# Modulation rows stored through one transposed 32 x 128 tile, and an issue-order edge on the weighted activations

## The chip, the cores and the metric

The kernel runs on one core of a Trainium2 chip. The metric is the device time of one execution in microseconds (us): 3135.5 us is the median of three runs before the change (3133.11 to 3138.17). The core has a matrix engine (TensorE, PE in the profile, with its weight loads as PEld), a vector engine (DVE), an activation engine (ACT), GpSimd (POOL) and a queue engine that mostly starts DMAs (SP). DMAs are also started from ACT and from POOL. Each engine works through its own instructions in the order in which they were queued, and the engines wait for each other through semaphores.

## The reference, cut to what matters

Two transformer blocks over 512 tokens of width 1024. The part that the change touches is the modulation of the first block: a vector `c` is turned into six vectors of 1024 numbers, three for the attention part and three for the expert part. The late four (`gt1`, `sh2`, `sc2`, `gt2`) are used after the attention.

```
mod_x = (silu(c) @ w_mod + b_mod)
sh1, sc1, gt1, sh2, sc2, gt2 = split(mod_x, 6)
px = split(modulate(rms_norm(x, norm1), sh1, sc1) @ w_in, ...)   # projections q, k, v, f, ...
x = x + gt1 * (concat([na_x, hg_x]) @ w_out)                       # attention and recurrence
x = x + gt2 * peer_ffn(modulate(rms_norm(x, norm2), sh2, sc2), ...)
```

`peer_ffn` picks 16 of 16384 experts for each token and head, and sums `gelu(u . h) * g * v` over them. The kernel computes it for 384 tokens as dense products with all experts, 128 chunks of 128 experts, with the weights `g` spread into a table of zeros; 128 tokens go through gathers.

## The kernel before, in words

`mixer` is the first stage. `mix_norm` normalises the input and makes the early modulation. Then `weave(self.project_na(first), self.late_mods())` runs two generators against each other: `project_na` projects q, k and v (each weight tile `w` of 512 KB or 256 KB comes by an SP DMA, ACT rounds it into `wh` at L148, DVE makes the rest `wl` at L149, PE multiplies at L122), and `late_mods` (L464 to L476) makes the four late vectors out of 32 chunks of 128 numbers. One chunk is `mod_chunk` (L326 to L333): an SP DMA of 512 KB into a buffer of the same ring `w` (four buffers, shared with the projection weights), one product with sum on DVE (L332, 1.22 us) and one small addition (L333).

A late vector lies as a column tile of 128 partitions x 8 numbers. It is also needed as a row (to be spread over all partitions later), so after every eight chunks `keep_rows` (L364 to L366) stores the column tile into a DRAM row `Rd[n]`, from POOL:

```
self.nc.gpsimd.dma_start(self.Rd[n].rearrange("(k p) -> p k", p=128), vec)
```

The target is contiguous along p and the source along k, so that no two neighbours of the source are neighbours in the target: one store is 1024 runs of 4 bytes. The rows are read back at L371 (`rows_of`), much later.

After the weave `lower_bounds` (L432 to L446) makes two small tables on DVE and ACT, and `project_f` (L592, matmuls at L611) is woven with `na_tiles` (`na_scores` L866 with the bias load L882, the score matmuls L887 and L890, the bias addition L892, the maximum L894 and the exponential L896; `na_transpose` L903; the value products).

What sets the order: the tile framework traces the instructions in program order and a scheduler places them on each engine; `with self.after(ins)` adds an edge that keeps what is traced inside behind `ins` on that engine's queue, without a wait. The expert loop at the end of `peer` calls `operands(e)` (L1376) for each chunk of 128 experts: the stored activations `act` are multiplied by the weights `Wr` on DVE (L1390), split into `sh` (ACT, L133) and `sl` (DVE, L135), and the weights `v` are split into `vh` and `vl` by the same helper `split` (L129 to L136).

Of the kernel before, what the change touches and what calls it, by code (L numbers as in the profile page):

```python
# [7 lines left out]
F32 = mybir.dt.float32  # L8
# [4 lines left out]
OP = mybir.AluOpType  # L13
# [3 lines left out]
D = 1024  # L17
S = 512
C = 256
KC = D // 128  # L20
# [6 lines left out]
GROUP = 8  # L27
# [24 lines left out]
def run(gen):  # L52
    while True:
        try:
            next(gen)
        except StopIteration as e:
            return e.value
# [7 lines left out]
def weave(*gens):  # L65

    at = [[0.0, i, g] for i, g in enumerate(gens)]
    while at:
        cur = min(at, key=lambda x: (x[0], x[1]))
        try:  # L70
            cur[0] += next(cur[2])
        except StopIteration:
            at.remove(cur)
# [18 lines left out]
class Net:  # L92
# [37 lines left out]
    def split(self, pool, src, shape, name, low=None, bufs=None):  # L130
        kw = {"bufs": bufs} if bufs else {}
        hi = pool.tile(shape, FR, name=name + "h", **kw)
        self.nc.scalar.activation(hi, src, AF.Copy)  # L133
        lo = pool.tile(shape, FR, name=name + "l", **kw)
        (low or self.nc.vector).tensor_tensor(out=lo, in0=src, in1=hi, op=OP.subtract)  # L135
        return hi, lo  # L136

    def rows2(self, src, k0, c0, n):
# [216 lines left out]
        self.nc.vector.tensor_tensor(out=m[:, n], in0=b[:, :4].rearrange("p (j i) -> p j i", j=2),  # L355
                                     in1=self.bm[:, n:n + KC + 1:KC].unsqueeze(2).to_broadcast([128, 2, 2]), op=OP.add)

    def gain_of(self, vec, scale, j, name):

        o = self.g.tile([128, KC], F32, name=name)  # L360
        self.nc.vector.scalar_tensor_tensor(o, scale[:, :, j], 1.0, self.gains[:, vec], op0=OP.add, op1=OP.mult)
        return o

    def keep_rows(self, n, vec):  # L364

        self.nc.gpsimd.dma_start(self.Rd[n].rearrange("(k p) -> p k", p=128), vec)  # L366

    def rows_of(self, n, name, pool):

# [5 lines left out]
    def mixer(self):  # L375
        y = self.pool("y")
        self.Y = y.tile([128, 4, 512], F32, name="Y")
        self.open_stream()
        pj = self.pool("pj")
        hh = pj.tile([128, KC, C + S], FR, name="hh")  # L380
        hl = pj.tile([128, KC, C + S], FR, name="hl")
        self.project_setup(pj, hh, hl)
        first = self.proj(self.p['win'], 0, 512, [self.xs])
        for n in self.mix_norm(hh, hl):
            if n % 2:
                next(first)
        m = self.pool("mixf", "right")
        self.F = m.tile([128, 2, 6, 512], F32, name="F")
        self.mixn = m = self.pool("mixn", "right")
        self.q2 = m.tile([128, 8, S], FR, name="q2")  # L390
        self.k2 = m.tile([128, 8, S + C], FR, name="k2")
        self.ql = m.tile([128, 4, S], FR, name="ql")
        self.V = m.tile([128, 9, 512], F32, name="V")
        weave(self.project_na(first), self.late_mods())
        with self.after(self.last_v):
            self.lower_bounds()
        self.shut("mp")
        na = self.pool("na", "right")
        weave(self.project_f(), self.na_tiles(na))
        self.shut("na")  # L400
        self.shut("mixn")
        m = self.pool("mixi", "right")
        self.I = m.tile([128, 6, 512], F32, name="I")
        self.G = m.tile([128, 4, 512], F32, name="G")
        self.hq = m.tile([128, 4, S], F32, name="hq")
        self.load_bounds()
        q = self.project_q()
        for _ in range(2):
            next(q)
        with self.after(self.last_exp):  # L410
            self.gates()
        run(q)
        self.shut("lbt")
        run(self.project_g())
        hg = self.pool("hg", "right")
        kv = []
        values = self.project_i()
        next(values)
        with self.after(self.log_table(self.last_sig)):
            weave(values, self.hg_keys_decayed(hg, kv))  # L420
        self.shut("pj")
        self.shut("st")
        self.hg_chunks(hg, kv)
# [38 lines left out]
                nc.vector.tensor_tensor(out=f, in0=f, in1=self.lb[:, d:d + 1].to_broadcast([128, 3, 512]), op=OP.add)  # L462

    def late_mods(self):  # L464
        self.Rd = self.tc.dram_tile([4, D], F32, name="Rd")
        for j, name in ((2, "gt1"), (3, "sh2"), (4, "sc2"), (5, "gt2")):
            t = self.g.tile([128, KC, 1], F32, name=name)
            setattr(self, name, t)
            for k in range(KC):
                self.mod_chunk(j, t[:, k], k)  # L470
                yield 3.0
            if j in (2, 3, 5):
                self.keep_rows((2, 3, 5).index(j) + (j > 2), t[:, :, 0])
            if j == 4:
                self.a2 = self.gain_of(1, t, 0, "a2")
                self.keep_rows(1, self.a2)  # L476

    def mix_norm(self, hh, hl):

# [548 lines left out]
    def peer(self):  # L1028
        nc, p = self.nc, self.p
        hh, hl = self.h2  # L1030
        mv = ([hh[:, k] for k in range(KC)], [hl[:, k] for k in range(KC)])
        first = self.proj_first(self.ws, mv, lambda i: self.normed_half(i, [(hh, hl, self.a2)], 1e-6, self.sh2[:, :, 0]))
        self.finish = None
        for name in ("wo", "st", "hca", "y", "pn"):
            self.shut(name)
# [56 lines left out]
        for t in range(4):  # L1092
            sq = self.sp.tile([128, 2], F32, name="ssp")
            for h in range(2):
                b = banks[t - 1][h] if t else self.accg[:, h * 512:(h + 1) * 512]
# [5 lines left out]
            r = self.rstd(sq, 1e-6)  # L1101
# [276 lines left out]
    def operands(self, pm, e, mv):  # L1378

        nc, p = self.nc, self.p  # L1380
        n, j = divmod(e, GROUP)
        if j == 0:
            self.Wr = self.Wn
        if e < AHEAD:
            a = pm.tile([128, TD], F32, name="act", bufs=3)
            nc.sync.dma_start(a, self.Ad[e])
        else:
            a = self.hidden(pm, self.rows_u(e), mv)
        a3 = a.rearrange("p (b t) -> p b t", t=WT)
        self.anchor = nc.vector.tensor_tensor(out=a3, in0=a3, in1=self.Wr[:, :, e % GROUP], op=OP.mult)  # L1390
        sh, sl = self.split(pm, a, [128, TD], "s", bufs=TAIL + OPS_LAG)
        v = self.st.tile([128, 2, 512], F32, name="w", bufs=WBUFS)
        nc.sync.dma_start(v.rearrange("p a b -> p (a b)"), p['V'][e])
        if j >= WLATE and e < 128 - GROUP:
            self.spread_rows(pm, n + 1, j - WLATE)
        vh, vl = self.split(pm, v, [128, 2, 512], "v", bufs=TAIL + OPS_LAG)
        return sh, sl, vh, vl
# [462 lines left out]
```

## Time and profile before

| | |
|---|---|
| runs before, median (lowest to highest) | 3135.5 us (3133.11 to 3138.17) |
| profiled execution, device time | 3140.31 us |
| its span, first to last instruction | 3138.5 us |
| PE busy | 2946.8 us, 94% of the span |
| DVE busy | 1890.9 us, 60% |
| ACT busy | 1271.9 us, 41% |
| POOL busy | 442.8 us, 14% |
| granted TensorE clock, mean | 0.969 |

The profiled execution is one execution; its own time is 4.8 us over the median, and the span is 1.8 us less than its time. Busy shares are means over stages of different kinds. The slices of the profile's page show PE at 90% or more nearly everywhere, and the slices in which it falls are short stages of their own; the first three (0 to 235 us) read 7, 8 and 7, and in the third the granted clock reads 8.

### The profile page before, as it was taken

The numbers are of one execution on the slowest core, as the hardware profiler recorded it, in microseconds if no ns is written. First come the engines' busy times: TensorE is split into PE (matmuls) and PEld (weight loads), VectorE is DVE, ScalarE is ACT, GpSimd is POOL, SyncE is SP. The second block draws the span as 40 slices with busy tenths as digits, with TensorE's granted clock in tenths as the row PEclk, the third lists the DMA queues.
The fourth block names the chain that finished last, engine by engine and source line by source line (L and its number), as shares of the span: only waits on it lengthen the run. The fifth ranks groups of instructions, "written<-read, shape, count | busy, mean of one in ns | idle before, by whom it ended". The sixth has DMA issues, their size and how long they took to land.

```text
span 3138.5 us, 42272 instructions
## 1 busy us (share of the span) xinstructions
PE 2946.8 (94%) x16009; PEld 2528.4 (81%) x16009; DVE 1890.9 (60%) x3640; ACT 1271.9 (41%) x2275; POOL 442.8 (14%) x402
## 2 busy tenths in 40 slices
PE   7879898999999999988898888899999999999998
PEld 5668797889899999967677777778888887788887
DVE  5644477639999966678788886544433245543323
ACT  4223464344366677633333323433323234433222
POOL 2200000100211210144454441000000000000000
PEclk9989999999999999999999999999999999999999
DMA  6832202334676776899999996222333222133332
GB/s 244 188 83 72 88 8 68 111 118 135 228 235 220 250 248 238 273 360 372 351 379 370 358 373 220 65 75 89 101 95 100 95 88 68 48 88 100 94 101 81
DMA packets 259148, 539.89 MB, mean 172 GB/s; under 512 B 21632, under 2 KB 136576, under 8 KB 254592
## 3 DMA queue, kind: packets, MB, share of 16 engines
q1 hardware_dynamic: 198368, 347.92, 34.9%
q0 software_dynamic: 36992, 134.25, 11.9%
q10 hardware_dynamic: 23584, 55.03, 4.7%
q8 instruction: 125, 2.05, 0.3%
q14 instruction: 79, 0.65, 0.1%
HBM read 487.02 MB, written 50.09 MB: 171 GB/s over the span
## 4 chain that ended last, share of the span: by engine, by line
PE 59%; DVE 18%; DMA 8%; issue 2%; ACT 1%; SPq 1%; POOL 0%; ACTq 0%; DVEq 0%; POOLq 0%
PE bank L122 57%; DMA act<-Ad 4%; DMA w<-in_V_dram 2%; DVE wl L1351 2%; DVE vl L135 2%; DVE gr L1163 2%; DVE accg L1168 2%; DMA gr<-in_Un_dram,iu 1%; DVE sl L135 1%; PE bank L611 1%; DVE act L1390 1%; PE bank L1499 1%; DVE tmp L1241 1%; DVE eq L1280 1%; DVE eq L1282 1%
## 5 line engine op out<-in xcount | busy, mean ns | idle before, releaser
L122 PE MATMUL bank<-hh,wl 128*128 128x512 f32 (+2 forms) x2304 | 840.5, 365 | 36.3 <-DVE wl L1351 18.4
L122 PE MATMUL bank<-hh,wh 128*128 128x512 f32 (+2 forms) x2304 | 845.4, 368 | 22.6 <-ACT wh L1350 8.8
L122 PE MATMUL bank<-hl,wh 128*128 128x512 f32 (+2 forms) x2304 | 834.4, 362 | 1.4 <-DVE hl L272 0.8
L149 DVE TENSOR_TENSOR wl<-w,wh 128x1024 fp32r<-128x1024 f32 (+2 forms) x280 | 297.1, 1062 | 644.6 <-ACT wh L148 637.6
L148 ACT ACTIVATE wh<-w 128x1024 fp32r<-128x1024 f32 (+2 forms) x280 | 257.4, 920 | 769.3 <-PE bank L122 596.8
L122 PEld LDWEIGHTS bank<-hh,wl 128*128 128x128 f32 x2304 | 439.3, 191 | 95.4 <-DVE wl L1351 26.7
L122 PEld LDWEIGHTS bank<-hh,wh 128*128 128x128 f32 x2304 | 438.7, 191 | 74.8 <-ACT wh L148 9.9
L122 PEld LDWEIGHTS bank<-hl,wh 128*128 128x128 f32 x2304 | 439.3, 191 | 50.8 <-DVE hl L272 1.5
L122 PE MATMUL bank<-vh,sh 128*128 128x512 f32 x768 | 251.5, 410 | 61.8 <-ACT sh L133 61.8
L1144 POOL DMA_INDIRECT gr<-in_Un_dram,iu x128 | 198.8, 1553 | 760.0 <-DVE accg L1168 523.5
L122 PE MATMUL bank<-vh,sl 128*128 128x512 f32 x768 | 245.8, 402 | 1.3 <-DVE sl L135 1.2
L122 PE MATMUL bank<-vl,sh 128*128 128x512 f32 x768 | 246.7, 403 | 0.0
L122 PEld LDWEIGHTS bank<-vh,sh 128*128 128x128 f32 x768 | 149.2, 198 | 102.4 <-ACT sh L133 72.9
L133 ACT ACTIVATE vh<-w 128x1024 fp32r<-128x1024 f32 x128 | 134.6, 1056 | 193.6 <-DMA w<-in_V_dram 169.5
L1351 DVE TENSOR_TENSOR wl<-w,wh 128x1024 fp32r<-128x1024 f32 x128 | 155.8, 1217 | 89.1 <-ACT wh L1350 89.0
L1350 ACT ACTIVATE wh<-w 128x1024 fp32r<-128x1024 f32 x128 | 135.3, 1058 | 153.9 <-PE bank L122 147.1
L122 PEld LDWEIGHTS bank<-vh,sl 128*128 128x128 f32 x768 | 148.6, 195 | 36.8 <-DVE sl L135 5.4
L122 PEld LDWEIGHTS bank<-vl,sh 128*128 128x128 f32 x768 | 149.3, 196 | 35.3 <-DVE vl L135 2.9
L1144 POOL DMA_INDIRECT gr<-in_V_dram,iv x128 | 161.0, 1258 | 83.9 <-DVE accg L1168 37.4
L216 POOL TENSOR_TENSOR r<-r,mhalf 128x1 f32<-128x1 f32 x37 | 21.9, 595 | 1014.1 <-DVE r L215 1007.3
L1168 DVE SCALAR_TENSOR_TENSOR accg<-gr,wt,accg 128x1024 f32<-128x1024 f32 x127 | 162.1, 1276 | 0.1
L135 DVE TENSOR_TENSOR vl<-w,vh 128x1024 fp32r<-128x1024 f32 x128 | 155.6, 1216 | 8.7 <-ACT vh L133 8.7
(367 smaller groups left out, 4719.2 us busy)
## 6 DMA issues: line engine op xcount, KB each, us to landing
w<-in_U_dram SPq DMA_DIRECT2D x128, 512.0 KB
w<-in_V_dram SPq DMA_DIRECT2D x128, 512.0 KB
w<-in_wgu_dram SPq DMA_DIRECT2D x84, 512.0 KB
Wd<-W ACTq DMA_DIRECT2D x24, 1024.0 KB
Wr<-Wd SPq DMA_DIRECT2D x96, 256.0 KB
w<-in_wdown_dram SPq DMA_DIRECT2D x44, 512.0 KB
Ad<-act ACTq DMA_DIRECT2D x116, 192.0 KB
act<-Ad SPq DMA_DIRECT2D x116, 192.0 KB
```

Source lines behind the costliest of these rows:

```text
L122: return self.nc.tensor.matmul(out, a, b, start=start, stop=stop)
L133: self.nc.scalar.activation(hi, src, AF.Copy)
L135: (low or self.nc.vector).tensor_tensor(out=lo, in0=src, in1=hi, op=OP.subtract)
L148: self.nc.scalar.activation(hi[:, :, :n], w[:, :, :n], AF.Copy)
L149: (self.low or self.nc.vector).tensor_tensor(out=lo[:, :, :n], in0=w[:, :, :n], in1=hi[:, :, :n], op=OP.subtract)
L611: nc.tensor.matmul(o, x[k], y[:, kk, :256], start=k == 0 and i == 0 and t % 2 == 0, stop=k == KC - 1 and i == 2, skip_group_check=True)
L1144: nc.gpsimd.indirect_dma_start(out=t, out_offset=None, in_=table, in_offset=bass.IndirectOffsetOnAxis(ap=idx, axis=0))
L1163: nc.vector.scalar_tensor_tensor(t, t, 1.0, self.h0, op0=OP.mult, op1=OP.mult, accum_out=dots[:, h, k:k + 1])
L1168: nc.vector.scalar_tensor_tensor(acc, t, wt[:, h, k:k + 1], acc, op0=OP.mult, op1=OP.add)
L1241: nc.vector.match_replace(tmp, val[:, 0:8], src, -3e38)
L1350: nc.scalar.activation(uh, w, AF.Copy)
L1351: nc.vector.tensor_tensor(out=ul, in0=w, in1=uh, op=OP.subtract)
```

## The change: one store of 32 rows, and an edge in the expert loop

The four late vectors become four slices of one tile `late` (128 partitions x 4 x 8). The four stores of 128 x 8 are gone. After the weave, `keep_rows` turns the whole tile with one transposing matmul against the identity into 32 partitions x 128, copies it from PSUM to `lr` on ACT, and stores it by one DMA from POOL: 32 pieces of 512 bytes. In `operands`, the weighted activations are traced inside `with self.after(self.last_low)`, where `last_low` is the last low part that `split` has made (in this place the `vl` of the chunk in front).

```diff
--- before.py
+++ after.py
@@ -132,7 +132,7 @@
         hi = pool.tile(shape, FR, name=name + "h", **kw)
         self.nc.scalar.activation(hi, src, AF.Copy)
         lo = pool.tile(shape, FR, name=name + "l", **kw)
-        (low or self.nc.vector).tensor_tensor(out=lo, in0=src, in1=hi, op=OP.subtract)
+        self.last_low = (low or self.nc.vector).tensor_tensor(out=lo, in0=src, in1=hi, op=OP.subtract)
         return hi, lo
 
     def rows2(self, src, k0, c0, n):
@@ -355,15 +355,14 @@
         self.nc.vector.tensor_tensor(out=m[:, n], in0=b[:, :4].rearrange("p (j i) -> p j i", j=2),
                                      in1=self.bm[:, n:n + KC + 1:KC].unsqueeze(2).to_broadcast([128, 2, 2]), op=OP.add)
 
-    def gain_of(self, vec, scale, j, name):
-
-        o = self.g.tile([128, KC], F32, name=name)
-        self.nc.vector.scalar_tensor_tensor(o, scale[:, :, j], 1.0, self.gains[:, vec], op0=OP.add, op1=OP.mult)
-        return o
-
-    def keep_rows(self, n, vec):
-
-        self.nc.gpsimd.dma_start(self.Rd[n].rearrange("(k p) -> p k", p=128), vec)
+    def keep_rows(self):
+
+        b = self.bank()
+        self.nc.tensor.transpose(b[:32, :128], self.late.rearrange("p n k -> p (n k)"), self.ident)
+        r = self.mp.tile([32, 128], F32, name="lr")
+        self.nc.scalar.copy(r, b[:32, :128])
+        self.Rd = self.tc.dram_tile([4, D], F32, name="Rd")
+        self.nc.gpsimd.dma_start(self.Rd.rearrange("n (k p) -> (n k) p", p=128), r)
 
     def rows_of(self, n, name, pool):
 
@@ -392,6 +391,7 @@
         self.ql = m.tile([128, 4, S], FR, name="ql")
         self.V = m.tile([128, 9, 512], F32, name="V")
         weave(self.project_na(first), self.late_mods())
+        self.keep_rows()
         with self.after(self.last_v):
             self.lower_bounds()
         self.shut("mp")
@@ -462,18 +462,14 @@
                 nc.vector.tensor_tensor(out=f, in0=f, in1=self.lb[:, d:d + 1].to_broadcast([128, 3, 512]), op=OP.add)
 
     def late_mods(self):
-        self.Rd = self.tc.dram_tile([4, D], F32, name="Rd")
-        for j, name in ((2, "gt1"), (3, "sh2"), (4, "sc2"), (5, "gt2")):
-            t = self.g.tile([128, KC, 1], F32, name=name)
-            setattr(self, name, t)
+        self.late = self.g.tile([128, 4, KC], F32, name="late")
+        sc2 = self.g.tile([128, KC, 1], F32, name="sc2")
+        self.gt1, self.a2, self.sh2, self.gt2 = (self.late[:, n] for n in range(4))
+        for j, t in ((2, self.gt1), (3, self.sh2), (4, sc2[:, :, 0]), (5, self.gt2)):
             for k in range(KC):
-                self.mod_chunk(j, t[:, k], k)
+                self.mod_chunk(j, t[:, k:k + 1], k)
                 yield 3.0
-            if j in (2, 3, 5):
-                self.keep_rows((2, 3, 5).index(j) + (j > 2), t[:, :, 0])
-            if j == 4:
-                self.a2 = self.gain_of(1, t, 0, "a2")
-                self.keep_rows(1, self.a2)
+        self.nc.vector.scalar_tensor_tensor(self.a2, sc2[:, :, 0], 1.0, self.gains[:, 1], op0=OP.add, op1=OP.mult)
 
     def mix_norm(self, hh, hl):
 
@@ -1029,7 +1025,7 @@
         nc, p = self.nc, self.p
         hh, hl = self.h2
         mv = ([hh[:, k] for k in range(KC)], [hl[:, k] for k in range(KC)])
-        first = self.proj_first(self.ws, mv, lambda i: self.normed_half(i, [(hh, hl, self.a2)], 1e-6, self.sh2[:, :, 0]))
+        first = self.proj_first(self.ws, mv, lambda i: self.normed_half(i, [(hh, hl, self.a2)], 1e-6, self.sh2))
         self.finish = None
         for name in ("wo", "st", "hca", "y", "pn"):
             self.shut(name)
@@ -1387,7 +1383,8 @@
         else:
             a = self.hidden(pm, self.rows_u(e), mv)
         a3 = a.rearrange("p (b t) -> p b t", t=WT)
-        self.anchor = nc.vector.tensor_tensor(out=a3, in0=a3, in1=self.Wr[:, :, e % GROUP], op=OP.mult)
+        with self.after(self.last_low):
+            self.anchor = nc.vector.tensor_tensor(out=a3, in0=a3, in1=self.Wr[:, :, e % GROUP], op=OP.mult)
         sh, sl = self.split(pm, a, [128, TD], "s", bufs=TAIL + OPS_LAG)
         v = self.st.tile([128, 2, 512], F32, name="w", bufs=WBUFS)
         nc.sync.dma_start(v.rearrange("p a b -> p (a b)"), p['V'][e])
```

On POOL, behind the casts of q (L561 before, L557 now), the four stores become one. Before, with `gt_647`, `sh_889`, `a_1252` and `gt_1255` as the four column tiles:

```order
L561 COPY q_578<-q_578 64x512
L366 DMA Rd<-gt_647 128x8x1
L366 DMA Rd<-sh_889 128x8x1
L366 DMA Rd<-a_1252 128x8x1
L366 DMA Rd<-gt_1255 128x8x1
L851 TENSOR_TENSOR r_4111<-r_4111,mhalf 128x2
```

The same place of the changed kernel, where `lr` is the transposed copy:

```order
L556 TENSOR_TENSOR ql<-F,q_578 64x512
L557 COPY q_578<-q_578 64x512
L365 DMA Rd<-lr 32x128
L847 TENSOR_TENSOR r_4109<-r_4109,mhalf 128x2
L847 TENSOR_TENSOR r_4248<-r_4248,mhalf 128x2
```

Three stores that stood inside the weave are gone, and the one that is left stands behind the last modulation chunk.

On PE, at the end of the v projection (its transposes are L585 and the 64 x 128 rows of L122), the first matmuls of `project_f` (L611) and the first scores (L887, L890). Before:

```order
L585 MATMUL bank<-ident,F 128x128 x16
L122 MATMUL bank<-ident,F 64x128 x24
L611 MATMUL bank<-wh,hh 128x256 x3
L887 MATMUL bank<-k_579,q_578 128x256 x2
L890 MATMUL bank<-k_579,ql 128x256 x2
L887 MATMUL bank<-k_579,q_578 128x256 x2
L890 MATMUL bank<-k_579,ql 128x256 x2
L611 MATMUL bank<-wl,hh 128x256
```

The same place of the changed kernel (`project_f` is L607 there, L361 is the new transpose):

```order
L581 MATMUL bank<-ident,F 128x128 x16
L122 MATMUL bank<-ident,F 64x128 x24
L361 MATMUL bank<-ident,late 32x128
L607 MATMUL bank<-wh,hh 128x256
L607 MATMUL bank<-wl,hh 128x256
L607 MATMUL bank<-wh,hl 128x256
```

The transpose of `late` now stands in front of all of `project_f`; the three first matmuls and the eight score matmuls that stood there come behind it (the scores after 36 matmuls of `project_f`).

On DVE, in the expert loop, one chunk of it. Before (L1390 is the weighting, L135 the low parts, L1163 and L1168 the gathered tokens):

```order
L1163 SCALAR_TENSOR_TENSOR gr,dots<-gr,h_5504 128x1024
L1390 TENSOR_TENSOR act<-act,Wr 128x384
L135 TENSOR_TENSOR vl<-w,vh 128x1024
L135 TENSOR_TENSOR sl<-act,sh 128x384
L1168 SCALAR_TENSOR_TENSOR accg<-gr,wt,accg 128x1024
```

And in the changed kernel, at the same place (rows 1908 to 1912 in both):

```order
L1159 SCALAR_TENSOR_TENSOR gr,dots<-gr,h_5502 128x1024
L1387 TENSOR_TENSOR act<-act,Wr 128x384
L135 TENSOR_TENSOR vl<-w,vh 128x1024
L135 TENSOR_TENSOR sl<-act,sh 128x384
L1164 SCALAR_TENSOR_TENSOR accg<-gr,wt,accg 128x1024
```

Only line numbers differ: DVE has 2777 rows in both kernels, and in the expert loop every one of them stands where it stood.

## Rows read from the trace of the kernel before

**Rows 1.** Busy time by stretches of 100 us: us, busy (instructions) by engine, clock, DMA.

```profile
100.00:200.00 100.00, 71.32 (x377) 58.93 (x375) 51.33 (x105) 17.57 (x31) 2.68 (x3) 0.80 0.68 153
```

**Rows 2.** Timeline of POOL, 92 to 175 us: start, us, engine, line, what, [idle before].

```profile
92.22 1.16 POOL L366 DMA_DIRECT2D Rd<-gt  x1
120.31 0.91 POOL L366 DMA_DIRECT2D Rd<-sh  x1 [26.93 <-DVE sh L333]
147.49 0.89 POOL L366 DMA_DIRECT2D Rd<-a  x1 [26.27 <-DVE a L361]
173.90 0.89 POOL L366 DMA_DIRECT2D Rd<-gt  x1 [25.53 <-DVE lbm L441]
```

**Rows 3.** Busy time by stretches of 4 us; the last two columns are DMA share, GB/s.

```profile
96.00:100.00 4.00, 4.00 (x25) 3.52 (x24) 1.39 (x3) 0.00 (x0) 0.00 (x0) 1.00 1.24 138
124.00:128.00 4.00, 4.00 (x20) 3.30 (x19) 0.40 (x3) 0.00 (x0) 0.00 (x0) 1.00 1.41 94
144.00:148.00 4.00, 4.00 (x12) 3.09 (x12) 3.08 (x8) 0.00 (x0) 0.51 (x1) 0.59 1.01 360
180.00:184.00 4.00, 3.78 (x32) 3.57 (x30) 0.00 (x0) 0.63 (x1) 0.00 (x0) 1.00 0.42 23
```

**Rows 4.** Waits from 55 to 180 us: engine, line, for what; total us, times, longest.

```profile
ACT wh L148 <- DMA w<-in_win_dram: 39.5, 3, 14.9
DVE mscr L332 <- DMA w<-in_wmt_dram: 34.1, 10, 11.9
```

**Rows 5.** Timeline of PE where it stood still, 100 to 192 us.

```profile
105.92 0.50 PE L122 MATMUL bank<-hh,wh 128*128 128x512 f32 x1 [3.96 <-ACT wh L148]
109.16 0.79 PE L122 MATMUL bank<-hh,wl 128*128 128x512 f32 x1 [2.36 <-DVE wl L149]
141.44 0.79 PE L122 MATMUL bank<-hh,wl 128*128 128x512 f32 x1 [5.45 <-DVE wl L149]
165.02 1.97 PE L122 MATMUL bank<-ident,F 128*64 128x128 f32 x16 [9.20 <-DVE V L577]
171.69 0.58 PE L611 MATMUL bank<-wl,hh 128*128 128x256 f32 x1 [0.97 <-DVE wl L149]
190.41 1.12 PE L903 MATMUL bank<-ident,P 128*128 128x128 f32 x4 [6.63 <-ACT P L896]
```

**Rows 6.** Timeline of PE in the v projection, two neighbouring matmuls at full clock.

```profile
150.43 0.39 PE L122 MATMUL bank<-hh,wl 128*128 128x512 f32 x1
150.66 0.39 PE L122 MATMUL bank<-wh,hh 128*128 128x512 f32 x1
```

**Rows 7.** Busy time from 94.96 to 164.28 us.

```profile
94.96:164.28 69.32, 49.10 (x233) 39.55 (x231) 35.58 (x73) 9.94 (x16) 1.79 (x2) 0.88 0.86 190
```

**Rows 8.** Timeline of DVE, 143 to 189 us.

```profile
143.32 1.23 DVE L332 SCALAR_TENSOR_TENSOR mscr<-w,crow 128x1024 f32<-128x1024 f32 x1 [0.53 <-DMA w<-in_wmt_dram]
145.57 1.23 DVE L332 SCALAR_TENSOR_TENSOR mscr<-w,crow 128x1024 f32<-128x1024 f32 x1 [0.82 <-DMA w<-in_wmt_dram]
...
149.79 1.22 DVE L332 SCALAR_TENSOR_TENSOR mscr<-w,crow 128x1024 f32<-128x1024 f32 x1
...
164.28 1.29 DVE L577 COPY V<-bank 128x512 f32<-128x512 f32 x2
...
173.47 0.14 DVE L333 TENSOR_TENSOR gt<-gt,bm 128x1 f32<-128x1 f32 x1
...
188.38 0.43 DVE L892 TENSOR_TENSOR bank<-bank,bias 128x256 f32<-128x256 f32 x1 [9.76 <-DMA bias<-in_nab_dram]
```

**Rows 9.** Busy time of three stretches around the start of project_f.

```profile
167.12:176.00 8.88, 7.91 (x36) 6.95 (x37) 7.54 (x20) 2.13 (x3) 0.89 (x1) 0.58 0.35 90
176.00:184.00 8.00, 7.78 (x65) 7.57 (x64) 0.69 (x1) 1.26 (x2) 0.00 (x0) 1.00 0.53 41
188.00:204.00 16.00, 13.60 (x74) 11.24 (x75) 7.40 (x13) 3.60 (x9) 0.00 (x0) 0.51 0.21 59
```

**Rows 10.** Timeline of ACT: the small store that stays.

```profile
174.79 0.38 ACTq L446 DMA_DIRECT2D Ld<-lbm  x1
```

## The prediction

> **What bounds the kernel now.** I read the busy time by stretches first, to see where PE, which is busy for 94% of the span, is not. From 100 to 200 us it is busy for only 71.32 us and its clock is granted at 0.80 [rows 1]. That is the weave of the q, k and v projections with the 32 late modulation chunks, and the start of project_f; both things that the change moves lie in it.
>
> The waits of that stretch come next. DVE waited 34.1 us for modulation weights and ACT 39.5 us for projection weights [rows 4]: both wait for loads. So I looked at when loads are slow. The four column stores are issued at 92.2, 120.3, 147.5 and 173.9 us [rows 2]. A few us behind each, the DMA engines are busy and move little: 138 GB/s at a share of 1.24, 94 GB/s at 1.41, 23 GB/s at 0.42 for the first, second and fourth, whereas between two stores they move 360 GB/s at 1.01 [rows 3]. (A share counts a packet's whole time where it starts, so it can pass 1.) The reader is to see the same thing three times at the same distance: some 4 to 10 us behind a 4 KB store, the 512 KB loads crawl.
>
> Last, PE's timeline: it stands still for 3.96 and 2.36 us, then 5.45, then 9.20, then 0.97 and 6.63 us [rows 5], 28.6 us in all. The first two lie behind store one, the third behind store two, the fourth behind store three (DVE reaches its copies of V late because its last chunks wait), and the last behind store four: the bias of the first scores comes 9.76 us late [rows 8]. After each stop PE runs at its lower level for a while: 0.59 and 0.58 where one of the stretches read 1.00 before [rows 3, 9].
>
> **The change part by part.**
>
> *The edge on the weighted activations: 0 us.* DVE's queue in the expert loop is the same, row for row, so the edge has nothing to move. No wait is added, since an edge of order on one engine needs none. The cost and the gain are nil; the second half of the change does not do what it says, because the order was already so.
>
> *Three stores leave the weave.* Take the moment at which DVE begins its copies of V, 164.28 us [rows 8], and ask when it could come without slow loads. PE's floor: k ends at 105.92 - 3.96 = 101.96 us [rows 5]; the v projection is 144 matmuls (four weight tiles of 36) at 150.66 - 150.43 = 0.227 us [rows 6], 32.7 us, so v ends at 134.7. DVE's floor: from 94.96 to 164.28 it works 35.58 us [rows 7], so it could be there at 130.5. The loads: between the stores, DVE took four chunks from 143.32 to 149.79 us [rows 8], 1.62 us each. The low part of the fourth v tile can't be made before PE leaves the second tile (101.96 + 16.4 = 118.4) and ACT has rounded the fourth, so about 121.2; nine chunks follow it, 14.6 us at that pace, and some 0.2 for the gain row: 136.0. Three engines and a ring of four buffers hand over to each other here, and I add 2 us for that: 138.0. The gain is 164.28 - 138.0 = 26.3 us. Bounds: at best PE's floor, 134.7 (29.6 us). At worst each of the 20 chunks in that stretch takes the slowest step between two stores, 145.57 - 143.32 = 2.25 us [rows 8], and none of DVE's other work (35.58 less 20 products of 1.23, 11.0 us) is beside it: 94.96 + 45.0 + 11.0 = 151.0 (13.3 us).
>
> *A transpose in front of project_f.* It waits for the last modulation addition, which in the trace comes 173.47 + 0.14 - 164.28 = 9.3 us behind the copies' start [rows 8]; queued behind it on PE is all of project_f and the scores. The trace has no such transpose; its nearest rows, the transposes in one group, are short, and I take 0.6 us for it and the hand-over, between 0.3 and 1. So project_f begins 9.9 us behind the copies, where before PE went on at 171.69 [rows 5], 7.4 us behind them, with 11 matmuls already done. On ACT the copy of the 32 rows stands in front of the small lower-bound store and the third weight tile of project_f, which has to wait until PE leaves the first (two buffers); it is hidden there. On SP nothing waits for the new store: its readers come hundreds of us later.
>
> *The fourth store becomes 32 rows.* The span from the copies' start to 204 us is 39.7 us before. PE's work in it, at full clock, is 7.91 x 0.58 + 7.78 x 1.00 + 13.60 x 0.51 = 19.3 us [rows 9]. After, I expect 9.9 us to project_f, these 19.3, the slow start that the first of these rows has already (7.91 x 0.42 = 3.3), and 0.5 for a bias that comes in time: 33.0. That is 6.7 us less, the new wait already paid for. Bounds: 8.2 less if the slow start halves. Nothing less (0) if the bias still comes late: then the 6.63 us stop and its slow stretch stay. The small lower-bound store of 256 runs at 174.79 [rows 10] stays, and it lies in the same disturbed stretch, so that a part of that disturbance may be its own.
>
> The new store is 32 runs instead of 4096 in four stores; by runs that is under a hundredth of the disturbance, and I take 0 (bound: as much as one old store, which is the case just named).
>
> The Trainium skill, page "DMA: Bandwidth & Descriptors", section "Measured (HBM→SBUF, 128 partitions, SWDGE, issued from GpSimd)", gives 0.68 us of DMA time for 4 KB. By it four stores are worth 2.7 us, and with the new wait (6.1 us, below) the time would be about 3138.9; the trace disagrees, with 94 GB/s in the stretch behind the second store [rows 3].
>
> **The sum.** 26.3 + 6.7 = 33.0 us. Nothing behind 204 us changes its order on any engine, so it comes through whole. The profiled execution took 3140.31 us, so its like would take 3107.3; the median before is 3135.5, and the forecast is 3102.5 us. The terms' bounds give 3135.5 - 29.6 - 8.2 = 3097.7 and 3135.5 - 13.3 - 0 = 3122.2.
>
> **The rivals.**
>
> *One disturbance stays.* The new store, or the small one beside it, slows the first loads of project_f and the bias as the fourth store did. For it: row 10 lies inside the fourth disturbed stretch. Against it: so few runs. The second term falls away: 3135.5 - 26.3 = 3109.2, up to 3122.2 with a slow first term.
>
> *The stores are cheap, and the loads crawl by themselves.* The stretch wants 512 KB every 1.3 us, and perhaps the DMA engines sag under that alone. Then the stops stay where they are, and only the new wait counts: project_f begins 2.5 us later, and the 11 matmuls (from 167.12 to 171.69 without the stop of 0.97: 3.6 us [rows 5, 9]) are no longer done in front of it: 3135.5 + 6.1 = 3141.6. For it: the waits are on loads, and the loads are dense. Against it: 360 GB/s between two stores at the same density, and the crawl begins a few us behind each of them. The price of a 4 KB transfer on the page of the Trainium skill named above speaks for this one.
>
> *PE pays for the transpose.* It is slower if the wait for the last modulation chunk decides: the loads stay as they are, PE stands for 7.2 us in one piece (from the end of the V transposes, 165.02 + 1.97 [rows 5], to 164.28 + 9.9), and a second slow start of 3.3 us follows: 6.1 + 3.3 = 9.4, 3144.9 us. It decides once the copies of V come less than 3 us earlier than before. For it: PE's order is strict here, and everything is behind the transpose. Against it: as above.
>
> **How the numbers follow.** What can be told from no change is about 0.2%, 6.3 us. The forecast, 80%, with its own range 3096 to 3112. One disturbance stays, 9%: still faster. Cheap stores, 6%: within 0.2%. PE pays, 5%: slower. So faster 0.89, same 0.06, slower 0.05. The range for 8 in 10 runs from 3094, a little below the terms' best, to 3122, the terms' worst.
>
> **What would show it.** Right: no stretch of the weave with the DMA share over 1 and under 150 GB/s; DVE's waits for modulation weights down from 34.1 to some 5 us; the copies of V begin between 135 and 141 us; PE stands for some 6 us in front of the transpose, and not at the first exponentials; the expert loop unchanged from its start to its end. Wrong: crawling loads that are still there without stores would overturn the first term; copies of V in time but a late first bias would overturn the second; a shift that is given back behind 204 us would show that something else sets the end.

## The result, and the profile after

The changed kernel takes 3104.1 us (median of four runs, 3098.0 to 3108.6) against 3136.6 us for the kernel before beside it (3133.1 to 3138.2): a ratio of 0.9893, 95% interval 0.9877 to 0.9909. The prediction was 3102.5 us. The profiled execution took 3106.44 us (span 3104.7, mean granted clock 0.978); the one before took 3140.31 (3138.5, 0.969). The gain is 32.5 us here. On another chip, in the experiments below, the changed kernel takes 3104.7 us as well, but the kernel before only 3128.7, so that the gain is 24.0 us there (ratio 0.9923, 0.9910 to 0.9937); the intervals of the two ratios don't overlap.

The stretch that the prediction started from, busy time by engine (columns as in [rows 1]); first 100 to 200 us, then two slices of 4 us in which the loads crawled before [rows 3], then a slice in the wait for the transpose, and last the start of `project_f`:

```profile
100.00:200.00 100.00, 89.58 (x672) 76.97 (x671) 63.86 (x129) 28.51 (x56) 0.78 (x1) 0.95 0.50 162
96.00:100.00 4.00, 4.00 (x25) 3.52 (x24) 1.40 (x3) 1.06 (x1) 0.00 (x0) 1.00 0.98 355
124.00:128.00 4.00, 4.00 (x19) 3.34 (x18) 2.33 (x5) 0.00 (x0) 0.00 (x0) 1.00 0.73 258
144.00:148.00 4.00, 0.00 (x0) 0.00 (x0) 4.00 (x9) 1.73 (x2) 0.00 (x0) 0.50 0.00 0
150.70:160.00 9.30, 9.30 (x60) 8.76 (x60) 2.83 (x7) 1.64 (x4) 0.78 (x1) 0.81 0.38 110
```

PE is busy for 89.58 us of the hundred, 71.32 before [rows 1]. At 96 and 124 us the DMA engines move 355 and 258 GB/s where it was 138 and 94 [rows 3]. In the slice at 144 us nothing is loaded and PE stands, but DVE is busy for all of it: it is DVE's own work that is waited for there (its copies of V, then the last modulation chunks), not a load.

DVE's waits for modulation weights from 55 to 180 us (engine, line, for what; total us, times, longest), 34.1 us before [rows 4]; ACT's for projection weights fell from 39.5 to 16.4 us:

```profile
DVE mscr L332 <- DMA w<-in_wmt_dram: 10.8, 10, 2.4
```

The timeline of PE where it stood still (as in [rows 5]), with the first `project_f` matmul and the first transposes of the exponentials:

```profile
141.60 1.09 PE L122 MATMUL bank<-ident,F 128*64 128x128 f32 x16 [1.56 <-DVE V L573]
150.25 0.39 PE L361 MATMUL bank<-ident,late 128*32 128x128 f32 x1 [7.55 <-DVE late L333]
150.35 0.55 PE L607 MATMUL bank<-wh,hh 128*128 128x256 f32 x1
...
160.31 0.60 PE L899 MATMUL bank<-ident,P 128*128 128x128 f32 x4
```

Six stops of 28.6 us in all [rows 5] have become four of 10.4 (0.20 and 1.11 us before the rows shown), and 7.55 of these are new: the wait of the transpose for the last modulation chunk. The first transposes of the exponentials no longer wait at all. DVE, the same moments as in [rows 8]:

```profile
140.85 1.29 DVE L573 COPY V<-bank 128x512 f32<-128x512 f32 x2
...
157.31 0.43 DVE L888 TENSOR_TENSOR bank<-bank,bias 128x256 f32<-128x256 f32 x1 [6.39 <-PE bank L886]
```

The copies of V begin 164.28 - 140.85 = 23.4 us earlier. A later fixed point is the load of the first late row (`gt1r`), after and before:

```profile
379.76 0.34 SPq L370 DMA_DIRECT2D gt1r<-Rd  x1
```

```profile
412.89 0.34 SPq L371 DMA_DIRECT2D gt1r<-Rd  x1
```

It is issued 33.1 us earlier. So 23.4 us come up to the copies of V, 9.7 between them and the read-back, and the end of the span (33.8 earlier) adds nothing of note. The new store, with the small store of the lower bounds next to it (ACT, at 150.94 us):

```profile
151.24 0.78 POOL L365 DMA_DIRECT2D Rd<-lr  x1 [59.03 <-ACT lr L363]
```

### The profile page after: what moved, and what is told of

The parts are those of the page before. It is cut to its first block, busy times and chain, and to the rows that moved or that the text cites. A ratio compares the mean times of both kernels' runs of the same rounds, so it can differ in the third digit from the quotient of the medians.

```text
span 3104.7 us, 42271 instructions
## 1 busy us (share of the span) xinstructions
PE 2929.6 (94%) x16010; PEld 2513.5 (81%) x16010; DVE 1890.6 (61%) x3640; ACT 1272.5 (41%) x2276; POOL 439.7 (14%) x399
## 3 DMA queue, kind: packets, MB, share of 16 engines
q0 software_dynamic: 36896, 134.25, 12.0%
q10 hardware_dynamic: 23584, 55.03, 4.8%
## 4 chain that ended last, share of the span: by engine, by line
PE 59%; DVE 17%; DMA 9%; issue 2%; ACT 1%; SPq 1%; POOL 0%; ACTq 0%; DVEq 0%; POOLq 0%
PE bank L122 57%; DMA act<-Ad 4%; DMA w<-in_V_dram 2%; DVE wl L1347 2%; DVE vl L135 2%; DMA gr<-in_Un_dram,iu 2%; DVE gr L1159 2%; DVE accg L1164 2%; PE bank L607 1%; DVE sl L135 1%; PE bank L1496 1%; DMA Wr<-Wd 1%; DVE act L1387 1%; DVE A L825 1%; DVE tmp L1237 1%
## 5 line engine op out<-in xcount | busy, mean ns | idle before, releaser
L122 PE MATMUL bank<-hh,wl 128*128 128x512 f32 (+2 forms) x2304 | 837.8, 364 | 28.2 <-DVE wl L1347 18.3
L122 PE MATMUL bank<-hh,wh 128*128 128x512 f32 (+2 forms) x2304 | 843.7, 367 | 19.4 <-ACT wh L1346 9.6
L122 PE MATMUL bank<-hl,wh 128*128 128x512 f32 (+2 forms) x2304 | 835.5, 363 | 1.0 <-DVE hl L531 0.5
L122 PEld LDWEIGHTS bank<-hh,wl 128*128 128x128 f32 x2304 | 439.0, 191 | 86.0 <-DVE wl L1347 26.9
L122 PEld LDWEIGHTS bank<-hh,wh 128*128 128x128 f32 x2304 | 438.2, 190 | 73.1 <-ACT wh L1346 10.5
L122 PEld LDWEIGHTS bank<-hl,wh 128*128 128x128 f32 x2304 | 439.1, 191 | 48.5 <-DVE hl L531 1.4
L122 PE MATMUL bank<-vh,sh 128*128 128x512 f32 x768 | 248.3, 405 | 63.1 <-ACT sh L133 63.1
L122 PE MATMUL bank<-vh,sl 128*128 128x512 f32 x768 | 244.8, 401 | 3.0 <-DVE sl L135 3.0
L122 PE MATMUL bank<-vl,sh 128*128 128x512 f32 x768 | 247.0, 404 | 0.0
L122 PEld LDWEIGHTS bank<-vh,sh 128*128 128x128 f32 x768 | 147.1, 195 | 103.9 <-ACT sh L133 74.8
L122 PEld LDWEIGHTS bank<-vh,sl 128*128 128x128 f32 x768 | 147.9, 195 | 39.1 <-DVE sl L135 8.0
L122 PEld LDWEIGHTS bank<-vl,sh 128*128 128x128 f32 x768 | 147.8, 194 | 35.4 <-DVE vl L135 4.1
L135 DVE TENSOR_TENSOR vl<-w,vh 128x1024 fp32r<-128x1024 f32 x128 | 155.9, 1218 | 8.7 <-ACT vh L133 8.7
```

The source lines that it names most:

```text
L122: return self.nc.tensor.matmul(out, a, b, start=start, stop=stop)
L135: self.last_low = (low or self.nc.vector).tensor_tensor(out=lo, in0=src, in1=hi, op=OP.subtract)
```

## The experiments

The theory: a store of 1024 runs of 4 bytes clogs the DMA engines, so that the 512 KB loads of the weave come late; the edge does nothing. Rivals: the loads crawl by themselves; the price is that of any store, or of POOL's queue; the gain came from PE's new order.

**The two parts apart.** One kernel is the kernel before with nothing but the edge, the other the changed kernel without the edge:

```diff
+        self.last_low = (low or self.nc.vector).tensor_tensor(...)   # in split
...
+        with self.after(self.last_low):
+            self.anchor = nc.vector.tensor_tensor(out=a3, ...)       # in operands
```

> The kernel before with the issue-order edge in the expert loop alone; the four column stores stay. Theory (the edge moves nothing, since DVE's queue is the same row for row): within 0.2% of the kernel before, 3130 to 3143 us. Rival (the edge is part of the gain): below 3130 us, in the extreme the whole 32 us.

> The changed kernel without the edge: only the one store of 32 rows. Theory: the whole gain is here, 3098 to 3110 us, ratio to the kernel before about 0.989. Rival (the edge is part of the gain): above 3110 us.

Measured on one chip, before at 3129.1 us: the edge alone 3128.3, ratio 0.9996 (0.9987 to 1.0005); the store alone 3105.1, ratio 0.9914 (0.9897 to 0.9931). The edge is worth nothing that can be measured, the store is worth all of the gain. The edge moves no instruction on any engine, so that the first of the two gives a second profile of the old order:

```profile
155.14 1.29 DVE L577 COPY V<-bank 128x512 f32<-128x512 f32 x2
```

Its copies of V begin 9.1 us earlier than those of the profile before (164.28 us [rows 8]), its late row is loaded at 399.5 us, and its span is 3124.8 us. With the store alone these are 137.41, 376.5 and 3102.8: of 23.0 us up to the read-back, 17.7 come up to the copies of V and 5.3 behind them.

**Put the three stores back.** Dummy stores into a DRAM tile that nothing reads, at the three places inside the weave where the column stores stood; the transpose and the one store of rows stay:

```diff
                 self.mod_chunk(j, t[:, k:k + 1], k)
                 yield 3.0
+            if j in (2, 3, 4):
+                self.nc.gpsimd.dma_start(self.Rx[j - 2].rearrange("(k p) -> p k", p=128), t)
```

> The changed kernel with three extra column stores (1024 runs of 4 bytes each, from POOL, into a DRAM tile that nobody reads) at the three places in the weave where the kernel before had them; the row store stays. Theory (the runs clog the DMA engines, and the loads behind them are late): the copies of V begin at 160 to 166 us again instead of 140.9, stretches with a DMA share near or over 1 at under 150 GB/s are back a few us behind each store, and the time is 26.3 us over the changed kernel by the first term, about 3125 to 3134. Rival (the loads crawl by themselves, or the gain is from PE's order): as the changed kernel, 3098 to 3110.

3124.4 us, ratio 0.9984 (0.9972 to 0.9995): 19.3 us over the store alone on the same chip. The rows of this kernel, slices of 4 us behind the three stores (issued at 90.12, 117.65 and 142.23 us), then the copies of V:

```profile
96.00:100.00 4.00, 3.86 (x23) 3.22 (x21) 0.00 (x0) 0.00 (x0) 0.00 (x0) 1.00 0.72 88
124.00:128.00 4.00, 4.00 (x19) 3.33 (x18) 0.00 (x0) 1.06 (x1) 0.00 (x0) 1.00 0.47 31
148.00:152.00 4.00, 1.89 (x32) 1.64 (x32) 0.00 (x0) 0.00 (x0) 0.00 (x0) 1.00 0.54 49
```

```profile
157.18 1.29 DVE L576 COPY V<-bank 128x512 f32<-128x512 f32 x2
```

DVE stands idle in each slice, the DMA engines are down to 31 to 88 GB/s, DVE's waits for modulation weights are 27.8 us (11.5 with the store alone), and the copies of V are back at 157.18 us (137.41 with the store alone). This is what three stores of 4 KB do, beside the same loads that run undisturbed without them. That the loads crawl by themselves is out. Time and copies come a little below what was expected (3125 to 3134 and 160 to 166 us), and the DMA share near or over 1 is not there: it reads 0.47 to 0.72. The trace also shows how long the stores themselves take: a median of 10.7 us from issue to landing for the two out of `late`, 3.9 for the 16 KB store of rows. By what step inside the DMA engines they hold up the loads is not shown.

**What of the store is it?** The same three places, the same 4 KB, with another layout or another queue:

```diff
-...rearrange("(k p) -> p k", p=128)               # 1024 runs of 4 bytes
+...rearrange("(p k) -> p k", p=128)               # e5: 128 runs of 32 bytes
+...rearrange("(k p i) -> p k i", p=128, i=2)      # e9: 512 runs of 8 bytes
+self.nc.scalar.dma_start(...)                     # e6: 1024 runs, from ACT
```

> The changed kernel once more, beside the three below, for comparison on one chip. Theory and rival alike: a ratio to the kernel before of about 0.989 to 0.991.

> The changed kernel with three stores of the same 4 KB from POOL at the three old places, into a DRAM tile that nothing reads, but laid out so that each is 128 runs of 32 bytes. Theory (the price goes by runs): an eighth of what the three column stores cost, about 2 to 3 us over the changed kernel, copies of V at 139 to 144 us, no stretch of the weave under 100 GB/s with work to load. Rival (a fixed price for every store from POOL in the middle of the loads): as with the three column stores, some 15 to 20 us, copies of V near 157.

> The changed kernel with the three column stores (1024 runs of 4 bytes each) at the three old places, started from ACT's queue instead of POOL's. Theory (the runs clog the DMA engines, whoever starts them): as from POOL, 15 to 20 us over the changed kernel, copies of V near 157 us, and stretches under 100 GB/s a few us behind each store. Rival (it is POOL's way of making descriptors that clogs): within 3 us of the changed kernel, apart from what issuing costs ACT.

> The changed kernel with three stores of 4 KB from POOL at the three old places, each 512 runs of 8 bytes. Theory (the price is in proportion to the runs; 1024 cost 19 us in three stores, 128 cost nothing that can be seen): about half, 7 to 11 us over the changed kernel, copies of V at 145 to 150 us. Rival (there is a store length that the ring of four buffers absorbs, and only what goes over it shows): 0 to 4 us, copies of V before 144 us.

The changed kernel itself came out at 3104.7 us, ratio 0.9923 (0.9910 to 0.9937). That ratio is above the 0.989 to 0.991 expected, because the kernel before is at 3128.7 us on this chip. With 128 runs per store: 3104.0, 0.9921 (0.9905 to 0.9937), copies of V at 137.54; not even the 2 to 3 us expected show. With 1024 runs from ACT: 3122.3, 0.9982 (0.9971 to 0.9992), copies of V at 158.46. With 512 runs: 3109.9, 0.9935 (0.9918 to 0.9952), copies of V at 145.05. Two slices of the kernel that stores from ACT, 7 and 5 us behind its first two stores:

```profile
96.00:100.00 4.00, 4.00 (x24) 3.43 (x22) 0.00 (x0) 0.00 (x0) 0.00 (x0) 1.00 0.30 37
124.00:128.00 4.00, 4.00 (x19) 3.34 (x18) 0.00 (x0) 0.00 (x0) 0.00 (x0) 1.00 1.00 68
```

Bytes, number of stores and place are the same in all of them, so it is the layout, and not POOL's queue: 17.7 us from ACT, nothing from POOL with 128 runs. The number of runs and their length change together here, and which of the two counts isn't separated. The Trainium skill, page "DMA: Bandwidth & Descriptors", section "Rules for kernel authors", says that a strided last dim lowers to one descriptor per element and that it should be rearranged to be contiguous, and that spreading DMAs over SP, ACT and GpSimd doesn't help, since all run on the same DMA engines. The runs agree with the second: 1024 elements cost about the same from either queue. On the first the profile's packet counts show it for ACT, whose queue carries 26704 packets for 23584, 1040 more for each store; POOL's queue carries 32 more for each store in all three layouts (36992 for 36896 with three), so that single elements can't be seen there. Whether the price is in proportion stays open: 512 runs cost 5.2 us, less than half of 17.7 to 19.3 and less than the 7 to 11 expected, but more than the rival's 4, and the intervals of 0.9935 and 0.9923 overlap.

**The fourth store alone.** One dummy column store behind the last modulation chunk, first in the changed kernel:

```diff
+            if j in (5,):
+                self.nc.gpsimd.dma_start(self.Rx[j - 2].rearrange("(k p) -> p k", p=128), t)
```

> The changed kernel with one extra column store behind the last modulation chunk, where the kernel before had its fourth. Theory: the copies of V stay near 141 us, but the bias of the first scores and the next weights of project_f are late again; the stop of 6.6 us and the slow clock behind it return, 7 to 13 us over the changed kernel, 3111 to 3117. Rival (the small lower-bound store beside it made the fourth disturbed stretch, and it is in both): no more than 3 us over the changed kernel.

3108.4 us, ratio 0.9924 (0.9906 to 0.9942), against 0.9914 without it on that chip: 3.3 us by the medians, the intervals overlap. The theory missed: the price is less than half of the 7 us expected at the least. DVE waits 2.85 us for a bias, and PE has no stop there. The disturbance itself is there: the small store of the lower bounds, from ACT's queue, takes 11.3 us to land where it took 3.9 without the column store. In the changed kernel the scores stand behind 36 matmuls of `project_f`, before behind three; PE has work for as long as the bias is late. To test that, the order had to come back without the store:

**The transpose moved behind project_f and the scores**, which restores the order of before on PE, and then with the fourth column store:

```diff
         weave(self.project_na(first), self.late_mods())
-        self.keep_rows()
...
         weave(self.project_f(), self.na_tiles(na))
+        self.keep_rows()
...
-        r = self.mp.tile([32, 128], F32, name="lr")     # in keep_rows
+        r = self.g.tile([32, 128], F32, name="lr")
```

The last two lines move the row tile into the pool `g`, since `mp` is closed by then.

> The changed kernel with the transpose, its copy and the store of 32 rows behind the weave of project_f and the scores instead of in front of it. Theory (PE's wait of 7.55 us for the last modulation chunk is the change's own cost, and what stood behind it can be done in it): PE goes on about 2.5 us earlier and has the first matmuls and scores of project_f behind it by then, 3.6 us of work: 4 to 6 us less than the changed kernel, ratio 0.987 to 0.988. Rival (the wait hides the loads of project_f, so that PE waits for these instead): within 2 us of the changed kernel, the stop of 7.55 us replaced by stops for loads or low parts of project_f's weights.

> The kernel with the transpose behind the weave of project_f (which has the old order of project_f and the scores), with one column store of 1024 runs behind the last modulation chunk, where the fourth stood. Theory (the order of the changed kernel, scores behind 36 matmuls, hid the late bias, so that the fourth column store cost only 2 to 3 us there; in the old order it costs its whole price): 6 to 10 us over the kernel with the later transpose, the bias waited for by 7 us or more, and a stop of PE of some 5 us at the first transposes of the exponentials. Rival (a fourth store alone costs little in any order, and the old stop came from three stores before it): 0 to 3 us, and no stop over 2 us there.

The later transpose alone: 3100.3 us (3096.4 to 3100.4), ratio 0.9907 (0.9893 to 0.9920), 4.4 us less than the changed kernel on the same chip; the runs of the two don't overlap (the changed kernel's fastest is 3101.5), though the intervals do. The 4 to 6 us expected are met; the ratio is not the 0.987 to 0.988 expected, again because of the kernel before on this chip. The load of `gt1r` is issued at 374.4 us, 378.6 in the changed kernel: the gain lies in front of it and not in where the moved tile lies. PE in that kernel, where it waits between V and `project_f`:

```profile
140.10 1.09 PE L122 MATMUL bank<-ident,F 128*64 128x128 f32 x16 [0.65 <-DVE V L573]
142.15 0.62 PE L607 MATMUL bank<-wh,hh 128*128 128x256 f32 x3 [0.96 <-ACT wh L148]
...
146.77 0.38 PE L607 MATMUL bank<-wl,hh 128*128 128x256 f32 x1 [2.43 <-DVE wl L149]
```

The stops are 4.0 us in place of 9.1, and eleven matmuls are done before the low part of the weights holds PE up. With the old order of PE and no column store the kernel is not slower than with the new order, so the gain doesn't come from the new order. With the fourth column store on top: 3107.6 us, ratio 0.9935 (0.9913 to 0.9956), 7.3 us more by the medians and 6.6 by the spans (3105.2, 3098.6); here too the runs don't overlap (its fastest is 3102.6), while the intervals just do. Its rows, DVE's first bias addition and PE's first transposes of the exponentials:

```profile
162.00 0.43 DVE L891 TENSOR_TENSOR bank<-bank,bias 128x256 f32<-128x256 f32 x1 [8.65 <-DMA bias<-in_nab_dram]
```

```profile
164.02 1.11 PE L902 MATMUL bank<-ident,P 128*128 128x128 f32 x4 [5.52 <-ACT P L895]
```

These are the rows of before again (9.76 and 6.63 us [rows 5, 8]). The same store costs about 7 us in the old order and some 3, not clear of the noise, in the new.

**Columns without a transpose, at a quieter time.** The late vectors are copied on ACT behind the last exponential of the scores, and four column stores go out of the copy from POOL at 282.6 us. In a second kernel the copy's tile is grown from 128 to 512 bytes a partition, and nothing else:

```diff
+        t = self.g.tile([128, 4, KC], F32, name="late2")               # e8
+        t = self.g.tile([128, 128], F32, name="late2")[:, :4 * KC]...  # e11
+        with self.after(self.last_exp):
+            self.nc.scalar.copy(t, self.late)
+        for n in range(4):
+            self.nc.gpsimd.dma_start(self.Rd[n].rearrange("(k p) -> p k", p=128), t[:, n])
```

> The changed kernel without the transpose: the late vectors are copied once on ACT behind the last exponential of the scores, and from that copy four column stores of 1024 runs each go out from POOL, one behind the other, behind project_f and the scores. Theory (a clogged stretch costs only where loads are needed just in time): within 6 us of the kernel with the transpose behind project_f, some 3097 to 3106 us, with a DMA stretch of some 35 us under 100 GB/s where little is loaded. Rival (4096 runs cost the same wherever they go): 20 us or more over it, 3120 us and up, as a wait of ACT or DVE for the weights of the next stage.

> The kernel of the four late column stores again, with its only new tile of 128 bytes a partition grown to 512 bytes, as much as the row tile has that the kernel with the later transpose keeps in the same pool, so that all tiles behind it lie where they lie there. No instruction moves on any engine. Theory (the stores cost the 7.9 us by which the lower bound's load is late, and the other 16 us came from matmuls that run 1.9% slower from 550 to 2500 us and behind, because the tiles lie 128 bytes further on): 3106 to 3110 us, and 219 matmuls of each kind from 2200 to 2350 us instead of 215. Rival (the 4096 runs slow everything behind them): 3120 us or more, and 215 matmuls of each kind there again.

The first took 3124.2 us, ratio 0.9984 (0.9973 to 0.9994), 24 us more than the kernel with the later transpose. Only a part of it is the stores' doing. DVE waits for the lower bounds, a load that ACT issues next to the stores:

```profile
298.42 3.43 DVE L461 TENSOR_TENSOR F<-F,om 128x1536 f32<-128x1536 f32 x2 [11.23 <-DMA om<-Ld]
```

With the later transpose that wait is 3.56 us, and the addition begins at 290.52: 7.9 us. The other 16 us gather over the rest of the kernel: from the issue of `gt1r` to the end of the span it takes 2740.2 us, and 2723.6 to 2729.3 in the thirteen other profiles of this document. Groups of instructions from 2200 to 2350 us, one of the three kinds of matmul that fill PE there, in the first kernel and then in the second:

```profile
L122 PE MATMUL bank<-hh,wh 128*128 128x512 f32 x215 | 85.0, 396 | 0.0
```

```profile
L122 PE MATMUL bank<-hh,wh 128*128 128x512 f32 x219 | 86.3, 394 | 0.0
```

215 of a kind against 219 in the same 150 us, 1.9% slower, with the instructions in the same order on every engine and a granted clock of 1.00 in both. That stretch is worth 2.7 us by itself. At the same matmul of both kernels the first is 2.0 us behind at 379 us, 12.0 at 1617, 8.6 at 1895 and 15.0 at the end, so the rest gathers unevenly, and whether all of it is these matmuls is not shown. The second kernel took 3113.6 us, on another chip, ratio 0.9946 (0.9927 to 0.9965): 0.0038 less than the first, 12 us. The count of matmuls came as the theory said; the time lies between the two expectations (3106 to 3110, and 3120 or more). So the rival (all of the 20 us and more from the stores) is out, and so is my first guess that quiet loads cost nothing: one load that was needed just then came 7.9 us late in the one kernel, and 12.94 us of wait stand there in the other. By the ratios the four late column stores still cost about 12 us over the later transpose (0.9946 for 0.9907).

## Why the prediction was right, step by step

The mechanism was right, and the time of the changed kernel too: 3104.1 us for 3102.5. That the sum fits so closely is partly luck. Two terms missed by about 3 us each, in opposite directions (23.4 for 26.3, 9.7 for 6.7), so that 33.1 us stand against 33.0. And both were sized on one profile of the kernel before in which the stores were dear: in the second profile of the old order the same terms are 17.7 and 5.3 us, inside the stated bounds (13.3 to 29.6, 0 to 8.2), and the gain on that chip is 24.0 us. Why the stores cost more in the one than in the other stays open.

*The edge, 0 us.* Right: 0.9996 (0.9987 to 1.0005).

*Three stores leave the weave, 26.3 us.* The mechanism was right, the size a little too large in this profile: 23.4 us. The copies of V came at 140.85 us for 138.0, inside the stated 135 to 141. In the other eight profiles without a 1024-run or 512-run store inside the weave they begin at 137.41 to 139.71 us, so 138.0 lies where these kernels lie, and this profile is the latest of them. What varies is the moment before: 164.28 us in the profile that the term was read from, 155.14 in the other. One size behind it was off: DVE's waits for modulation weights fell from 34.1 to 10.8 us [rows 4], not to some 5. I had taken 1.62 us a chunk from a short run of four and put 2 us on top for the hand-over; how much of the difference the 2 us covered was not measured. The first sign of being right (no stretch with a DMA share over 1 and under 150 GB/s) came true but proves little, since with three stores put back the share stayed at 0.72 and less in the slices shown.

*The transpose.* Right: `project_f` begins at 150.35, 9.5 us behind the copies (9.9 predicted), and PE stands for 7.55 us (some 6 predicted). The later transpose showed its price, 4.4 us by the medians, where the sum had 6.1 as the cost of the new wait.

*The fourth store, 6.7 us.* Measured 9.7. Of the 3.0 us more, 0.4 are the earlier `project_f`, 0.5 the bias that I allowed for and that isn't waited for, and 1.5 the slow start: 9.30 us at a granted clock of 0.81 lose 1.8 us, where I had kept 3.3 [rows 9]; 0.6 stay open. (The bound with half the slow start should read 8.4 us, not 8.2.) What I said of the cause holds only in part. I put the old stop down to the store; the runs show that it took the store and the old order together (6.6 to 7.3 us and the stop with both, some 3 us and no stop with the store in the new order, no stop at the exponentials in the old order without the store). The transpose in front, which I counted as a cost alone, also puts 33 more matmuls ahead of the scores.

*The new store, 0 us.* Right as far as can be seen: PE has no stop from 151.24 to 192 us, and the small store of the lower bounds beside it [rows 10] does no harm there either.

*The rivals.* "One disturbance stays" is out by the bias, which is in time. "The stores are cheap" is out by the three stores put back, 19.3 us. "PE pays for the transpose" describes a wait that is there, 7.55 us, and its condition failed by far: the copies came 23.4 us earlier (17.7 against the second profile of the old order) and not less than 3. Nothing was given back behind 204 us.

## What to carry to other kernels

Look at the runs of a small transfer, not at its bytes alone: three 4 KB stores in 1024 runs each cost this kernel 17.7 to 19.3 us, in 128 runs nothing that could be measured, and the wait stood under the name of the loads. Look a few us behind each such store for slices with few GB/s while an engine waits for a load; the DMA share is no sign, it read from 0.30 to 1.41 in such slices. A price that is read from one profile may be that profile's own: up to the read-back the change gained 33.1 us against one profile of the old order and 23.0 against another. A transpose on PE is a cheap way out, but it takes a place in PE's order: put it where what it waits for has long been done.

## What was not expected of the hardware

A tile of 128 bytes a partition in place of one of 512, with no instruction moved, went with 128x512 matmuls that were 1.9% slower in a stretch of a later stage (215 against 219 of a kind in 150 us) and a kernel 12 us longer by the ratios. It is one pair of kernels, on two chips; which address of which operand does it was not tried. It also means that an experiment that adds a tile can measure its layout and not its edit. The dummy stores above add no SBUF tile.
